# One VectorE operation in an activation, the first pair of units started beside the last single one, and other buffer counts in the merge

## Chip, cores, metric

The kernel runs on one core of a Trainium2 chip. The metric is the device time of one execution in microseconds (us); for each kernel the median of several runs is given. A profile is one execution of its own, taken with the hardware profiler. TensorE is called PE here, its weight loads PEld, VectorE DVE, ScalarE ACT, GpSimd POOL and the queue that starts most transfers SP (SPq in rows). L213 means line 213 of the kernel before.

## What is computed

One step of a hybrid decoder layer, for a prompt of 1024 tokens and for 8 samples of 4 new tokens each with 2048 past tokens in a paged cache. The part that the change touches is the compressed-block branch and what follows the attention:

```python
def compress(k, pe, w1, w2):
    # blocks of 32 positions every 16: two chunks of 16 positions make a block
    proj = jnp.einsum('bckx,mxh->mbckh', chunks, w1r)
    hid = pe.reshape(-1) @ w1
    for m in range(CMP_RATIO):
        hid = hid + proj[m, :, m:m + n_cmp]
    return jax.nn.gelu(hid) @ w2

def merge_and_mlp(x, a, c, ga, gb, w_nsa_out, w_conv_out, w_o, g_mlp, w_up, w_down):
    m = jax.nn.sigmoid(ga) * (a @ w_nsa_out) + jax.nn.sigmoid(gb) * (c @ w_conv_out)
    x = x + m @ w_o
    h = rms_norm(x, g_mlp)
    return x + jnp.square(jax.nn.relu(h @ w_up)) @ w_down
```

`compress` is applied to the keys and values of the prompt and of each of the 8 samples: 18 units. The samples' attention then uses compressed blocks, selected blocks gathered from the cache, and a window.

## The kernel before

Every product in float32 is made of three products of rounded halves (`mm3`, L212 to L215), so a tile that enters a product is first split: a cast on ACT gives the high part, a subtraction on DVE the low part. The kernel is written with a planner: each engine executes its instructions in one fixed order, which the planner derives before the run from the order of the program and from its own estimate of when each is ready. A buffer count (`bufs=`) says how many tiles of a tag live at once; a tile beyond it waits for the release of an earlier one.

The stages in order of time: projections and short convolution (to 325 us), the prompt's attention beside the gates' products (to 840 us), six single sample units among it, five pairs of sample units beside the samples' attention (865 to 1087 us), the merge of the branches (to 1172 us), the product with w_o in two halves of columns (to about 1270 us), the MLP up and down (to the end).

A single sample unit (`comp_unit`, L528) gathers its rows from the cache by a POOL transfer (`gth`), orders them by head (`gpr`, DVE, one of four quarters on POOL), transposes them on PE (`ct`), splits them (`cth`, `ctl`) and multiplies by w1 into `hid`. It stops at a first `yield`; then ACT adds the bias into the tile `x` (named gx, L592), and after a second `yield` `blocks_out` (L488) follows: Square on ACT (L492), two operations on POOL (L493, L494), Tanh on ACT (L495), one operation on DVE (L496), the product with w2 on PE (`kvc`, L513 or L519) and a copy out of PSUM (L515 or L526). `compress` (L705) starts a unit, then finishes the one before it by `finish` (L711), so that the chain of one unit lies beside the products of the next.

A pair (`pair_unit`, L646) handles two samples with shared weight sums. It has three stages of products, n = 0, 1, 2, with a `yield` after each. The loop at L1332 goes over five pairs; after stage 0 it finishes the unit before, and after each stage it advances the generator `probs`, the samples' attention, by some steps. `probs` consists of 62 steps: 21 for the softmax weights of each group of four samples (window keys `swn` transposed into `skT`, selected rows `gk` gathered on POOL, weights written to DRAM as `sl_d`), then 10 for the values of each group (weights read back into `skt`, products `so`). The step counts come from

```python
            for _ in range(SSTEP[i + n % 2] * 2 // 3):
                next(probs, None)
```

with values 6 and 7, so 4 steps after each stage, 12 for a pair. Before the loop stand, in this order, `finish()` at L1324 (the last single unit), the closing of its pools, the opening of the pools for the pairs and of another PSUM layout, and the loading of weight sums.

The merge goes over 8 tiles of 128 output channels, j = 0 to 7. For each, `load_merge` (L1291) brings the gate `ta` and the conv branch `cg` (EB buffers each), `load_wn` (L1298) the weights `wnr`, which are split into `wnh` and `wnl`. Of the split weights two slots serve j = 0, 1, 3, 4, 6, 7 and one serves j = 2, 5. `merge_in` multiplies (`na`, three column banks), adds on DVE (L1376) and POOL (L1377), and L1397, L1398 split the result (`mT`). `load_wo` (L1400) loads and splits eight tiles for each half of w_o, with WOB buffers and two raw ones (`wor`).

Of the kernel before, what the change touches and what calls it, by code (L numbers as in the profile page):

```python
# [11 lines left out]
F32 = mybir.dt.float32  # L12
# [3 lines left out]
AF = mybir.ActivationFunctionType  # L16
OP = mybir.AluOpType
# [29 lines left out]
CJ = (1, 3)  # L47
W1S = 4
UGP = 1
EB = 3  # L50
XTB = 5
ATT = dict(lg=3, pt=2, pv=1, gx=1, gy=1)
PB = 12
WOB = 9
QB = 12
WB = 2
GB = 2
# [6 lines left out]
HALVES = (slice(0, 512), slice(512, D))  # L64
QTB = 2
PTB = 2
UG = 1
TORDER = (0, 1, 2, 3, 8, 4, 5, 6, 7)
NP0 = 4
SDOWN = {**{p: (p - 1,) for p in range(1, 11)}, 11: (10, 11), 12: (12, 13), 13: (14, 15)}  # L70
WUB = 6
CB = 2
SADV = [2] * 10
SSTEP = [0, 0, 0, 0, 0, 0, 6, 6, 6, 6, 6, 6, 6, 6, 6, 7]
SKT = 5
GPRP = (3,)
GK = 4
# [43 lines left out]
def tile_hybrid_step(ctx, tc, xp, xs, cck, ccv, csk, csv, swk, swv, sconv, ptab, g_attn, w_in,  # L121
# [366 lines left out]
    def blocks_out(kv, x, t, n, b):  # L488

        prompt, nv = b is None, 2 * n - 2  # L490
        xv, tv = x[:, :, :nv], t[:, :, :nv]
        S.activation(tv, xv, AF.Square)  # L492
        P.tensor_scalar(tv, tv, 0.044715, 1.0, op0=OP.mult, op1=OP.add)  # L493
        P.tensor_mul(tv, tv, xv)  # L494
        S.activation(tv, tv, AF.Tanh, scale=GC)  # L495
        V.scalar_tensor_tensor(xv, tv, 1.0, xv, op0=OP.add, op1=OP.mult)  # L496
        xh = x.rearrange("p m (c h) -> p m c h", h=2)
        w2 = w2t[kv]
        nblk = n - 1
        po = ps(HT["ct"], "kvc")  # L500
        if kv == "k":
            if prompt:
                for h in range(2):
                    for mt in range(2):
                        PE.matmul(po[:, h * 64:h * 64 + nblk], w2[:, mt].rearrange("p a d -> p (a d)"),
                                  xh[:, mt, :nblk, h], start=mt == 0, stop=mt == 1)
                pv = po[:, :128].rearrange("p (h c) -> p h c", h=2)[:, :, :nblk]
                S.copy(pkh[:, :, :nblk], pv)
                V.tensor_sub(pkl[:, :, :nblk], pv, f32(pkh[:, :, :nblk]))
            else:  # L510
                for h in range(2):
                    for mt in range(2):
                        PE.matmul(po[h * 64:h * 64 + 64, :nblk], w2[:, mt, 0, :], xh[:, mt, :nblk, h],  # L513
                                  start=mt == 0, stop=mt == 1)
                V.tensor_copy(kcT[:, b, :], po[:, :nblk])  # L515
        else:
            for h in range(2):
                for mt in range(2):
                    PE.matmul(po[:nblk, h * 64:h * 64 + 64], xh[:, mt, :nblk, h], w2[:, mt, 0, :],  # L519
                              start=mt == 0, stop=mt == 1)  # L520
            if prompt:
                pv = po[:nblk, :128].rearrange("p (h d) -> p h d", h=2)
                S.copy(pvc[:nblk, :, 0, :], pv)
                V.tensor_sub(pvc[:nblk, :, 1, :], pv, f32(pvc[:nblk, :, 0, :]))
            else:
                V.tensor_copy(vcN[:, b, :], po[:nblk, :128])  # L526

    def comp_unit(kv, w1, cv, n, b):  # L528


        cols = 2 * n
        prompt = b is None
        hid = ps(HT["hid"], "hid")
        pieces = []
        for lp2 in range(4):
            hi = up.tile([128, 2, 256], F32R, name="cth", tag="cth", bufs=CB)
            lo = up.tile([128, 2, 256], F32R, name="ctl", tag="ctl", bufs=CB)
            pt = ps(HT["ct"], "ct")
            pv = pt[:, :2 * cols].rearrange("p (i c h) -> p i c h", i=2, h=2)
            part = cv(lp2)  # L540
            for i in range(2):
                for h in range(2):
                    PE.transpose(pv[:, i, :, h], part[:, h, i * 128:i * 128 + 128], ident[:n, :n])
            pf = pt[:, :2 * cols].rearrange("p (i c) -> p i c", i=2)
            if prompt:

                for m in range(2):
                    c = slice(m * 128, m * 128 + cols - 2)
                    src = pf[:, :, 2 * m:2 * m + cols - 2]
                    S.copy(hi[:, :, c], src)  # L550
                    V.tensor_sub(lo[:, :, c], src, f32(hi[:, :, c]))
                    c = slice(m * 128 + cols - 2, m * 128 + cols)
                    src = peT[kv][:, m * 8 + 2 * lp2:m * 8 + 2 * lp2 + 2]
                    src = src[:, :, None].to_broadcast([128, 2, 2])
                    V.tensor_copy(hi[:, :, c], src)
                    V.tensor_sub(lo[:, :, c], src, f32(hi[:, :, c]))
            else:
                S.copy(hi, pf)  # L558
                V.tensor_sub(lo, pf, f32(hi))
            pieces.append((hi, lo))  # L560
        if prompt:
            for i in range(16):
                m, lp = i % 2, i // 2
                k = m * 8 + lp
                hi, lo = (z[:, lp % 2, m * 128:m * 128 + 128] for z in pieces[lp // 2])
                PE.matmul(hid[:, :256], hi, w1[k][0], start=i == 0, stop=False)
                PE.matmul(hid[:, :256], hi, w1[k][1], start=False, stop=False)
                PE.matmul(hid[:, :256], lo, w1[k][0], start=False, stop=i == 15)
            turned = up.tile([128, 2, 256], F32, name="gx", tag="gx", bufs=UGP if prompt else UG)[:, 0]
            V.tensor_copy(turned, hid[:, :256])  # L570
            hid = ps(HT["hid"], "hid")
            hv = hid[:, :256].rearrange("p (m c) -> p m c", m=2)
            for mt in range(2):
                PE.transpose(hv[:, mt], turned[:, mt * 128:mt * 128 + 128], ident)
        else:
            hv = hid.rearrange("p (m c) -> p m c", m=2)
            nn = cols - 2
            for mt, i in MTI:
                m, lp = i % 2, i // 2
                k = m * 8 + lp  # L580
                hi, lo = (z[:, lp % 2, 2 * m:2 * m + nn] for z in pieces[lp // 2])
                ws = slice(mt * 128, mt * 128 + 128)
                mm3(hv[:, mt, :nn], w1[k][0][:, ws], w1[k][1][:, ws], hi, lo, i == 0 and mt == 0, i == 15 and mt == 1)
        yield
        pb = pbias[kv]
        if prompt:
            V.tensor_copy(pb, hv[:, :, cols - 2])
        nv = cols - 2
        x = up.tile([128, 2, 256], F32, name="gx", tag="gx", bufs=UGP if prompt else UG)
        t = up.tile([128, 2, 256], F32, name="gt", tag="gt", bufs=UGP if prompt else UG)  # L590
        for mt in range(2):
            S.activation(x[:, mt, :nv], hv[:, mt, :nv], AF.Identity, bias=pb[:, mt:mt + 1])  # L592
        yield
        blocks_out(kv, x, t, n, b)
# [51 lines left out]
    def pair_unit(kv, cache, b0, w1):  # L646
# [15 lines left out]
            xs.append(xt.rearrange("p i (j e h) -> p i j e h", e=2, h=2))  # L662
        x = u2.tile([128, 2, 512], F32, name="gx2", tag="gx2", bufs=1)
        xo = x.rearrange("p m (j e h) -> p m j e h", e=2, h=2)
        mid = u2.tile([128, 2, 256], F32, name="mid", tag="mid", bufs=1)
        pb = pbias[kv]
        for n in range(3):
            hid = ps(HT["hid"], "hid")
# [26 lines left out]
                             mid[:, :, :2 * nj].rearrange("p m (j h) -> p m j h", h=2))  # L695
        yield
        for s_ in range(2):
            t = u2.tile([128, 2, 256], F32, name="gt", tag=("gt", "mid")[s_], bufs=1)
            blocks_out(kv, x[:, :, s_ * 256:s_ * 256 + 256], t, 128, b0 + s_)

    behind = []
# [596 lines left out]
    def load_wn(j, raw=None):  # L1298

        if raw is None:  # L1300
            raw = ep.tile([128, 4, 128], F32, name="wnr", tag="wnr", bufs=1)
        DMA.dma_start(raw, w_nsa[0, :, j * 128:(j + 1) * 128].rearrange("(k p) c -> p k c", p=128))
        pool, n = (wp, 2) if j % 3 < 2 else (ep, 1)
        h, l = (pool.tile([128, 4, 128], F32R, name="wn" + x, tag="wn" + x, bufs=n) for x in "hl")
        S.copy(h, raw)
        V.tensor_sub(l, raw, f32(h))
        return h, l
# [13 lines left out]
        compress(sample_unit("k", cck, i, w1), ("k", i))  # L1321
        advance(STEP[i])
    advance(100)
    finish()  # L1324
    close("unit", "pa", "cTh")
    s1 = open_pool("s1", "right", bufs=2)
    up = u2 = open_pool("u2", "right")
# [4 lines left out]
    for i in range(ATTEND + 1, 2 * NB, 2):  # L1332
# [4 lines left out]
        for n in range(3):  # L1337
            next(unit)
            if n == 0:
                finish()  # L1340
            for _ in range(SSTEP[i + n % 2] * 2 // 3):
                next(probs, None)
            if i == 2 * NB - 2:
                if n == 0:
                    close("w2")
                    ap_ = open_pool("aT", "left")
                    aTh = ap_.tile([128, 4, T], F32R, name="aTh")
                    aTl = ap_.tile([128, 4, T], F32R, name="aTl")
                    wp = open_pool("w", "left")
                    wns = []  # L1350
                if n < 2:
                    load_aT(n)
                    wns.append(load_wn(n, room()[:, 0].rearrange("p (k c) -> p k c", k=4)))
                else:
                    for qi in (2, 3):
                        load_aT(qi)
# [492 lines left out]
```

## Time and profile before

| what | value |
|---|---|
| median of 3 runs | 1959.02 us (1954.49 to 1960.22) |
| the profiled execution, its own time | 1965.28 us |
| span of its instructions | 1963.5 us |
| PE busy | 1898.9 us, 97% |
| DVE, ACT, POOL busy | 1129.9, 859.0, 443.8 us |
| mean granted PE clock | 0.985 |

Engines work side by side, so the busy times do not add up to the span. An engine's idle time matters only where the others wait for it. The granted clock of PE is 1.0 at full speed (2.4 GHz) and 0.5 at its lower level (1.2 GHz); a stretch with a value between has a part at either.

### The profile page before, as it was taken

The numbers are of one execution on the slowest core, as the hardware profiler recorded it, in microseconds if no ns is written. First come the engines' busy times: TensorE is split into PE (matmuls) and PEld (weight loads), VectorE is DVE, ScalarE is ACT, GpSimd is POOL, SyncE is SP. The second block draws the span as 40 slices with busy tenths as digits, with TensorE's granted clock in tenths as the row PEclk, the third lists the DMA queues.
The fourth block names the chain that finished last, engine by engine and source line by source line (L and its number), as shares of the span: only waits on it lengthen the run. The fifth ranks groups of instructions, "written<-read, shape, count | busy, mean of one in ns | idle before, by whom it ended". The sixth has DMA issues, their size and how long they took to land.

```text
span 1963.5 us, 34847 instructions
## 1 busy us (share of the span) xinstructions
PE 1898.9 (97%) x13172; PEld 1766.6 (90%) x13172; DVE 1129.9 (58%) x2375; ACT 859.0 (44%) x1905; POOL 443.8 (23%) x626
## 2 busy tenths in 40 slices
PE   9999999999999999989899989999999999999998
PEld 8999998999998989876778877799999999999998
DVE  5324232454446666657775452498676755667765
ACT  5113223555546555545444230365454444443333
POOL 3112223443444444433232340130000000000000
PEclk9999999999999999989999999999999999999999
DMA  6465326222236521165536454337666656755654
GB/s 207 128 160 135 94 62 157 79 60 69 75 73 206 174 98 52 47 197 186 164 123 209 169 190 143 123 107 253 230 208 222 214 210 225 251 184 166 186 194 158
DMA packets 236312, 303.77 MB, mean 155 GB/s; under 512 B 20661, under 2 KB 163142, under 8 KB 232048
## 3 DMA queue, kind: packets, MB, share of 16 engines
q1 hardware_dynamic: 229232, 267.99, 43.9%
q0 software_dynamic: 6912, 33.56, 4.9%
q8 instruction: 104, 1.70, 0.4%
q14 instruction: 64, 0.52, 0.1%
HBM read 222.78 MB, written 78.71 MB: 154 GB/s over the span
## 4 chain that ended last, share of the span: by engine, by line
PE 70%; DMA 5%; DVE 4%; ACT 2%; POOL 1%; issue 1%; SPq 0%; DVEq 0%; POOLq 0%; ACTq 0%
PE c L213 9%; PE c L214 9%; PE c L215 9%; PE PT L942 3%; PE ga L214 3%; PE ga L213 3%; PE ga L215 3%; PE hid L214 2%; PE hid L215 2%; PE hid L213 2%; DMA wrd<-sd_d 2%; PE pv L949 2%; PE pv L948 2%; PE so L1234 1%; PE sl L1195 1%; PE skT L1103 1%
## 5 line engine op out<-in xcount | busy, mean ns | idle before, releaser
L213 PE MATMUL c<-ud,whd 128*128 128x264 f32 x768 | 218.5, 287 | 6.8 <-ACT whd L1645 4.3
L214 PE MATMUL c<-ud,whd 128*128 128x264 f32 x768 | 218.2, 286 | 0.0
L215 PE MATMUL c<-ud,whd 128*128 128x264 f32 x768 | 218.2, 286 | 0.0
L868 POOL TENSOR_SCALAR P<-P,st,gates 128x256 f32<-128x256 f32 (+4 forms) x272 | 150.2, 569 | 127.2 <-DVE st L864 104.6
L213 PEld LDWEIGHTS c<-ud,whd 128*128 128x128 f32 x768 | 145.1, 190 | 7.2 <-ACT whd L1645 4.5
L213 PE MATMUL c<-hBt,wuh 128*128 128x264 f32 x512 | 146.1, 285 | 2.3 <-ACT p L1534 2.3
L215 PE MATMUL c<-hBt,wul 128*128 128x264 f32 x512 | 146.3, 286 | 0.0
L214 PEld LDWEIGHTS c<-ud,whd 128*128 128x128 f32 x768 | 145.8, 190 | 0.0
L215 PEld LDWEIGHTS c<-ud,whd 128*128 128x128 f32 x768 | 145.1, 190 | 0.0
L946 DVE TENSOR_TENSOR ptl<-PT,pth 128x512 fp32r<-128x512 f32 (+1 forms) x148 | 99.5, 686 | 65.7 <-ACT pth L945 65.3
L1645 ACT CAST whd<-wrd 128x512 fp32r<-128x512 f32 x112 | 68.3, 621 | 152.2 <-issue 97.3
L213 PE MATMUL ga<-hTh,whu 128*128 128x384 f32 (+1 forms) x384 | 128.4, 334 | 0.0
L214 PE MATMUL ga<-hTl,whu 128*128 128x384 f32 (+1 forms) x384 | 127.0, 331 | 0.0
L215 PE MATMUL ga<-hTh,wlu 128*128 128x384 f32 (+1 forms) x384 | 126.6, 330 | 0.0
L236 POOL TENSOR_TENSOR wlu<-wru,whu 128x1024 fp32r<-128x1024 f32 x32 | 76.7, 2397 | 216.3 <-ACT whu L235 216.3
L1646 DVE TENSOR_TENSOR whd<-wrd,whd 128x512 fp32r<-128x512 f32 x112 | 76.5, 691 | 84.3 <-ACT whd L1645 84.0
L945 ACT CAST pth<-PT 128x512 fp32r<-128x512 f32 (+1 forms) x148 | 83.7, 588 | 67.8 <-PE PT L942 64.4
L214 PE MATMUL c<-h2r,wuh 128*128 128x264 f32 x384 | 109.6, 285 | 0.3 <-POOL h2r L1560 0.2
L213 PE MATMUL hid<-cth,w1h 128*128 128x254 f32 (+1 forms) x352 | 102.6, 292 | 2.7 <-ACT cth L558 1.9
L214 PE MATMUL hid<-ctl,w1h 128*128 128x254 f32 (+1 forms) x352 | 103.8, 295 | 1.4 <-DVE ctl L682 1.4
L942 PE MATMUL PT<-cst,P 128*128 128x128 f32 (+1 forms) x592 | 101.0, 274 | 0.2 <-DVE st L923 0.2
L215 PE MATMUL hid<-cth,w1l 128*128 128x254 f32 (+1 forms) x352 | 99.7, 283 | 0.0
(540 smaller groups left out, 5949.2 us busy)
## 6 DMA issues: line engine op xcount, KB each, us to landing
ur<-u_d SPq DMA_DIRECT2D x96, 264.0 KB
wru<-in_w_up SPq DMA_DIRECT2D x36, 512.0 KB
u_d<-u SPq DMA_DIRECT2D x64, 264.0 KB
wru<-in_w_in SPq DMA_DIRECT2D x32, 512.0 KB
h2r<-in_w_down SPq DMA_DIRECT2D x32, 512.0 KB
sd_d<-h2r SPq DMA_DIRECT2D x16, 1024.0 KB
wrd<-sd_d SPq DMA_DIRECT2D x64, 256.0 KB
wrd<-in_w_down SPq DMA_DIRECT2D x48, 256.0 KB
```

The source lines that it names most:

```text
L213: PE.matmul(out, wh, ah, start=first, stop=False)
L214: PE.matmul(out, wh, al, start=False, stop=False)
L215: PE.matmul(out, wl, ah, start=False, stop=last)
L236: (leng or P.tensor_sub)(l, raw, f32(h))
L868: P.tensor_scalar(p, p, self.st[:, br, 3, g:g + 1], gates[:, self.qi, 3 * hg + br:3 * hg + br + 1], op0=OP.mult, op1=OP.mult)
L942: PE.transpose(pt[:n, g * 128:(g + 1) * 128], pg[g], ident)
L945: S.copy(hi[:n], pt[:n])
L946: V.tensor_sub(lo[:n], pt[:n], f32(hi[:n]))
L948: PE.matmul(self.o, w, hi[:n], start=first and i == 0, stop=False)
L949: PE.matmul(self.o, w, lo[:n], start=False, stop=last and i == len(tiles) - 1)
L1645: S.copy(h, raw)
L1646: lows.append(V.tensor_sub(l, raw, f32(h)))
```

## The change

It makes five edits. In `blocks_out` the two POOL operations become one DVE operation, with the constants moved into the scale of Tanh; t·(1 + 0.044715·t²) is written as 0.044715·t·(t² + 1/0.044715). `finish()` ahead of the pairs becomes one step of the waiting unit, up to its second `yield`, and the unit is finished after stage 0 of the first pair; for this its tiles `gx` and `gt` move into the pool `cmp`, which stays open, and the pair's `mid` and second `gt` share them. The steps of `probs` become 5, 4 and 4 after the stages, 13 for a pair. `ta` and `cg` get four buffers in place of three, `wnr` two in place of one. The split tiles of w_o get eight in place of nine.

```diff
-EB = 3
+EB = 4
-WOB = 9
+WOB = 8
-UG = 1
-SSTEP = [0, 0, 0, 0, 0, 0, 6, 6, 6, 6, 6, 6, 6, 6, 6, 7]
+SSTEP = (5, 4, 4)
@@ blocks_out
         S.activation(tv, xv, AF.Square)
-        P.tensor_scalar(tv, tv, 0.044715, 1.0, op0=OP.mult, op1=OP.add)
-        P.tensor_mul(tv, tv, xv)
-        S.activation(tv, tv, AF.Tanh, scale=GC)
+        V.scalar_tensor_tensor(tv, tv, 1 / 0.044715, xv, op0=OP.add, op1=OP.mult)
+        S.activation(tv, tv, AF.Tanh, scale=0.044715 * GC)
@@ comp_unit
-            turned = up.tile([128, 2, 256], F32, name="gx", tag="gx", bufs=UGP if prompt else UG)[:, 0]
+            turned = up.tile([128, 2, 256], F32, name="tu", tag="tu", bufs=UGP)[:, 0]
-        x = up.tile([128, 2, 256], F32, name="gx", tag="gx", bufs=UGP if prompt else UG)
-        t = up.tile([128, 2, 256], F32, name="gt", tag="gt", bufs=UGP if prompt else UG)
+        x, t = (mp.tile([128, 2, 256], F32, name=nm, tag=nm, bufs=1) for nm in ("gx", "gt"))
@@ pair_unit
-        mid = u2.tile([128, 2, 256], F32, name="mid", tag="mid", bufs=1)
+        mid = mp.tile([128, 2, 256], F32, name="mid", tag="gx", bufs=1)
-            t = u2.tile([128, 2, 256], F32, name="gt", tag=("gt", "mid")[s_], bufs=1)
+            t = mp.tile([128, 2, 256], F32, name="gt", tag=("gt", "gx")[s_], bufs=1)
@@ load_wn
-            raw = ep.tile([128, 4, 128], F32, name="wnr", tag="wnr", bufs=1)
+            raw = ep.tile([128, 4, 128], F32, name="wnr", tag="wnr", bufs=2)
@@ ahead of the pairs
     advance(100)
-    finish()
+    next(behind[0][0])
     close("unit", "pa", "cTh")
@@ loop over the pairs
-            for _ in range(SSTEP[i + n % 2] * 2 // 3):
+            for _ in range(SSTEP[n]):
                 next(probs, None)
```

## Rows read from the trace of the kernel before

**Rows 1.** The page: busy us of each engine, share of the span, instructions.

```profile
PE 1898.9 (97%) x13172; PEld 1766.6 (90%) x13172; DVE 1129.9 (58%) x2375; ACT 859.0 (44%) x1905; POOL 443.8 (23%) x626
```

**Rows 2.** Waits of PE, 840 to 1110 us: for whom, us, times, longest.

```profile
PE kvc L513 <- DVE gx L496: 5.3, 1, 5.3
PE so L1234 <- DMA skt<-sl_d: 3.7, 1, 3.7
PE skT L1103 <- DMA swn<-in_state_win_k: 3.1, 1, 3.1
```

**Rows 3.** Waits of PE, 1110 to 1165 us.

```profile
PE na L213 <- ACT wnh L1305: 10.9, 3, 4.1
```

**Rows 4.** PE in order of time, 857 to 871 us: start, us, operation [idle before].

```profile
863.03 1.12 PE L513 MATMUL kvc<-gx,w2k 128*64 128x127 f32 x8 [5.29 <-DVE gx L496]
864.56 1.97 PE L660 MATMUL ct<-cst,gpr 128*128 128x128 f32 x8 [0.40 <-DVE kcT L515]
...
870.31 0.36 PE L213 MATMUL hid<-cth,w2h 128*128 128x256 f32 x1
```

**Rows 5.** DVE in order of time, 857 to 865 us.

```profile
858.46 0.28 DVE L515 COPY kcT<-kvc 128x127 f32<-128x127 f32 x1
```

**Rows 6.** Seven stretches: length, busy us per engine, granted PE clock, DMA share, GB/s.

```profile
864.15:870.31 6.16, 5.76 (x46) 5.24 (x45) 3.75 (x12) 2.52 (x5) 2.68 (x8) 0.55 1.01 349
1114.82:1118.41 3.59, 0.00 (x0) 0.00 (x1) 3.54 (x9) 2.70 (x7) 2.26 (x2) 1.00 0.00 0
...
1129.26:1132.47 3.21, 0.00 (x1) 0.00 (x1) 2.21 (x4) 2.09 (x4) 0.24 (x1) 1.00 0.39 130
1132.47:1136.00 3.53, 3.53 (x12) 3.47 (x13) 3.53 (x6) 1.68 (x4) 2.23 (x2) 0.52 0.60 194
1145.91:1149.98 4.07, 0.01 (x1) 0.00 (x1) 2.90 (x7) 1.66 (x3) 2.65 (x3) 0.94 1.06 391
1149.98:1153.00 3.02, 3.02 (x10) 3.02 (x11) 1.40 (x2) 0.45 (x1) 0.43 (x1) 0.51 0.70 251
...
1050.17:1057.40 7.23, 7.23 (x36) 6.33 (x38) 1.53 (x4) 0.39 (x1) 0.00 (x0) 0.53 0.08 24
```

**Rows 7.** Two lines of the kernel: operation, count, ns min/median/max, start of first and last.

```profile
L494 POOL TENSOR_TENSOR gt<-gt,gx x18: 730/1275/1594, 213.6 to 1094.5; 128x508 f32<-128x508 f32 x16, 128x252 f32<-128x252 f32 x2
L496 DVE SCALAR_TENSOR_TENSOR gx<-gt,gx x18: 422/680/1158, 214.8 to 1098.0; 128x508 f32<-128x508 f32 x16, 128x252 f32<-128x252 f32 x2
```

**Rows 8.** Stages of pairs and of w_o's turn: length, PE, PEld, DVE, ACT, POOL busy, clock, DMA.

```profile
870.50:1087.00 216.50, 206.55 (x1463) 162.46 (x1461) 151.10 (x282) 101.75 (x192) 70.26 (x67) 0.98 0.55 177
...
1216.90:1237.40 20.50, 19.40 (x81) 14.40 (x80) 9.38 (x12) 5.40 (x9) 1.70 (x4) 1.00 0.35 109
```

**Rows 9.** DVE and POOL in order of time, 912 to 919 us.

```profile
915.69 2.17 DVE L481 TENSOR_TENSOR w1l<-w1r,w1h 128x512 fp32r<-128x512 f32 x1
...
918.12 0.68 DVE L481 TENSOR_TENSOR w1l<-w1r,w1h 128x512 fp32r<-128x512 f32 x1
...
916.03 1.28 POOL L494 TENSOR_TENSOR gt<-gt,gx 128x508 f32<-128x508 f32 x1
```

**Rows 10.** The SP queue in order of time, 1100 to 1141 us: start and length of issues.

```profile
1101.48 1.69 SPq L1404 DMA_DIRECT2D wor<-in_w_o  x2
1119.41 0.38 SPq L1302 DMA_DIRECT2D wnr<-in_w_nsa_out  x1
...
1140.40 0.60 SPq L1302 DMA_DIRECT2D wnr<-in_w_nsa_out  x1
```

**Rows 11.** ACT in order of time, 1114 to 1150 us.

```profile
1114.90 0.52 ACT L1397 ACTIVATE mT0h<-ta 128x384 fp32r<-128x384 f32 x1 [18.48 <-PE ownT L1256]
...
1149.31 0.62 ACT L1305 CAST wnh<-wnr 128x512 fp32r<-128x512 f32 x1 [0.25 <-DVE ta L1376]
```

**Rows 12.** ACT in order of time, 1213 to 1220 us.

```profile
1213.69 1.14 ACT L1407 CAST woh<-wor 128x512 fp32r<-128x512 f32 x2 [41.71 <-PE wo L226]
1218.22 1.27 ACT L1407 CAST woh<-wor 128x512 fp32r<-128x512 f32 x2 [3.39 <-DMA wor<-in_w_o]
```

## Prediction

> **What bounds the kernel now.** First the page: PE is busy for 1898.9 of 1963.5 us [rows 1]. DVE, the next engine, is busy 58% of the span. So only two things shorten this kernel: PE standing idle for less time, or PE running for less time at its lower clock. The change takes no product away. The next view is therefore PE's waits over the stages that the change touches. From 840 to 1110 us, which holds the last single unit and the five pairs, three waits matter: 5.3 us for the activation chain of the last single unit, 3.7 us for a weight read back from DRAM, and 3.1 us for a window tile [rows 2]. In the merge there are three waits of 10.9 us together, all for the split of `wnh` [rows 3]; in order of time they are 3.59, 3.21 and 4.07 us, as the stretches without PE in [rows 6] show. The last view is the granted clock just behind such waits. It is 0.51 to 0.55 for the next 3 to 7 us [rows 6], the lower level for nearly all of the stretch, and a wait costs that as well: 3.53 x 0.48 = 1.7 us in the stretch from 1132.47 us, 3.02 x 0.49 = 1.5 us from 1149.98 us, 7.23 x 0.47 = 3.4 us from 1050.17 us.
>
> **The unit finished behind stage 0.** Now PE has nothing to do between the last single unit's products and its `kvc`, which start at 863.03 us after 5.29 us of waiting; the first transposes of the pair (`ct`) stand behind them in PE's fixed order and start at 864.56, the pair's first products (`hid`) at 870.31 us [rows 4]. In the changed order `ct` comes first. What it still needs is the PSUM bank that the unit before used, free when the copy L515 ends at 858.46 + 0.28 = 858.74 us [rows 5]; its data had been ordered by head before that. So `ct` should start near 858.8 in place of 864.56 us, 5.8 us earlier. The eight `kvc` products are not gone, they come back behind stage 0 with up to the 1.1 us that they took [rows 4]. Term: 5.8 - 1.1 = 4.7 us gained. Bounds: 0, if the loading of the weight sums is late next; and 5.29 + 0.40 + 6.16 x 0.45 = 8.5 us, if the stretch at clock 0.55 [rows 6] also runs at full speed and nothing else does its waiting. The moved chain adds a wait: `mid` shares its buffer with the unit's `gx`, so the bias on ACT (L692) waits for `kvc`, and behind it on ACT queue the casts `cth` for stage 1, for which PE waits. At most that is the same 1.1 us, once. The unit issues no transfers after its start, so none is moved. On POOL's queue the first four gathers of `gk` stand behind L494 of this unit; without it they can go sooner, and no wait of PE is put down to them [rows 2].
>
> **The activation.** It goes over 18 units. POOL loses two operations in each, the larger with a median of 1.275 us [rows 7]; POOL is busy for 70.3 of 216.5 us in the pairs [rows 8] and bounds nothing there. DVE gains one operation of a form and size that it already runs in L496, median 0.680 us [rows 7]: 16 x 0.68 + 2 x 0.42 = 11.7 us over the kernel, of which ten, 6.8 us, lie in the pairs. There DVE is busy for 151.1 of 216.5 us [rows 8] and would rise from 70 to 73%. The price is on the path where the new operation, waiting for Square on ACT, stands ahead of a `ctl` on DVE's queue for which PE waits. Bounds: 6.8 us lost, if each of the ten delays PE by its full length; and 0.6 us gained, the difference once, since the chain itself is shorter (at least 1.28 us of POOL against 0.68 of DVE, and the 10 chains overlap other work). I take 1 us lost: DVE is idle for over a quarter of the stage, and PE's queue there has other work ready.
>
> What speaks for less: where L494 runs on POOL, a DVE subtraction beside it took 2.17 us and the same form without it 0.68 us [rows 9]. The Trainium skill, SBUF — State Buffer, Who interferes with whom, says that a DVE instruction with two inputs in SBUF blocks fully against a POOL instruction that reads SBUF, whichever starts second. The trace agrees. The same rule also speaks against the edit, since the new operation has two such inputs and can itself be held by POOL's remaining work; by it the term would be nearer to 0 than to 1 us lost.
>
> **The steps of probs.** No work is added: the steps that do something stay 62, and they come up to five earlier in program order at the end of the pairs. What can change is what PE meets in its queue. The 3.7 us wait is for a transfer of weights, the 3.1 us wait for a window tile [rows 2], both transfers of SP whose place in the order moves. Bounds: both waits and their clock gone, 3.7 + 3.1 + 3.4 + 1.6 = 11.8 us (1.6 as in the other short waits); or as much again added. I take 0, because the length of those transfers and the number of their buffers stay.
>
> **Four merge tiles, two raw weight buffers.** The load of `wnr` for j = 3 is issued at 1119.41 us, when the split of j = 2 has freed the one raw buffer; SP had issued its last load ahead of it by 1103.17 [rows 10]. PE's wait of 3.21 us for its cast ends at 1132.47 us [rows 3, 6]. With a second buffer the load can follow the others at about 1102, 17 us sooner. What is late next is the slot for the split tile, which j = 0 leaves when its last bank is multiplied. PE's last products before the wait end at 1129.26 us [rows 6], and j = 1 and 2 each have a bank after that of j = 0, so the slot is free a few us before it is needed. For j = 5 the load goes at 1140.40 us [rows 10], the cast at 1149.31 [rows 11], and the wait is 4.07 us [rows 6]; its load stands on SP's queue behind loads of `ta` and `cg` that wait for one of three buffers, and the fourth buffer lets those go a tile sooner. Both gone: 3.21 + 4.07 + 1.7 + 1.5 = 10.5 us, with the clock from above. The first wait, 3.59 us, stays: its cast stands on ACT behind `mT`, which had waited 18.48 us until 1114.90 [rows 11], and no buffer count changes that. Bounds: 0, if the casts keep their places in ACT's order behind `mT`; 10.5 + 3.59 + 1.6 = 15.7 us, if the planner also turns the first. I take 9.
>
> **Eight tiles of w_o.** With nine, one tile of the second half of w_o is split ahead of time; with eight all wait for the last products of the first half. The casts then go in twos, the second two 4.5 us after the first [rows 12]. PE is idle for 1.1 of 20.5 us there now [rows 8]. One more tile late is half of such a turn, 2.3 us, part of it covered by the products of three row blocks that are open at once. Bounds: 0 and 4.5; I take 1.5 us lost.
>
> **Sum.** -4.7 + 1.0 + 0 - 9.0 + 1.5 = -11.2 us. The profiled execution took 1965.28 us (span 1963.5) and would take 1954.1; it lies 6.3 us above the median of the runs. From that median, 1959.02 - 11.2 = 1947.8, so 1948 us.
>
> **Rivals.** A measurement of this kernel can tell about 0.3%, 6 us, from no change: under 1953 is faster, above 1965 slower.
> (1) Forecast: the chain at the first pair and two of three waits of the merge go. 1948, its own range 1939 to 1955. 0.60.
> (2) The merge keeps its waits: the casts stay behind `mT` and the loads of w_o on ACT, and the earlier landing is worth nothing. For it: the first of the three waits is already of that kind [rows 11]. Against: the load of j = 3 starts only at 1119.41. Then -4.7 + 1.0 + 1.5 = -2.2, 1957 us. 0.18.
> (3) Slower: the denser steps put products of `probs` that wait for a transfer ahead of the pairs' own on PE's fixed queue, in each pair instead of in two of the five. Three more such waits of 3.4 us with 2.5 us of clock are 17.7 us, the sum is +6.5 and the time 1965.5. It decides from two such added waits on. For it: both waits there now are of this kind [rows 2]. Against: most steps find their data. 0.10.
> (4) More: the planner's new order also removes the first wait of the merge (5.2 us) and one of the two in the pairs (about 6): -22, 1937 us. 0.12.
> The range from 1935 to 1960 holds (1), (2), and most of (4). Chances: faster 0.69 (nearly all of (1), and (4)), same 0.20 ((2) and the rest of (1)), slower 0.11.
>
> **What the profile after would show.** `ct` of the first pair within 2 us behind the last single unit's products, and `kvc` of that unit behind the 48 products of the pair's stage 0, with no wait for L496. No L493 or L494 work on POOL. `wnr` for j = 3 issued right behind the first three pairs of `ta` and `cg`, and one wait of PE for `wnh` in place of three, with clock 1.0 from 1120 us on. In w_o, eight casts after the last product of the first half. I am wrong if waits for `ctl` appear in each pair, if the pairs' stage (216.5 us, less what the first pair gains) grows, or if the casts of `wnh` still stand behind `mT`.

## The result and the profile after

The changed kernel takes 1941.98 us (median of 6 runs, 1940.09 to 1948.32), the kernel before 1959.62 us (6 runs, 1954.49 to 1965.02). The ratio is 0.9917, with a 95% interval of 0.9894 to 0.9940: 16.3 us less, between 11.8 and 20.8. The forecast was 11.2 us less, 1948 us. The time lies in the range and the direction is right, but three of the five terms behind it are not (the first pair, the steps of `probs` and the tiles of w_o), as the runs below show.

The profiled execution of the changed kernel took 1940.09 us, its lowest time, and that of before 1965.28 us, above all six runs counted here. The two traces are therefore 25.2 us apart where the medians are 17.6 apart. Sizes of stages are read from the traces, verdicts from the ratios.

The page of the changed kernel, answering to [rows 1]:

```profile
PE 1885.6 (97%) x13172; PEld 1753.9 (91%) x13172; DVE 1132.3 (58%) x2393; ACT 857.6 (44%) x1905; POOL 412.3 (21%) x590
```

PE runs the same 13172 products in 13.3 us less: it spends less time at the lower clock. DVE has 18 instructions more, POOL 36 fewer. Cutting both spans at the same products shows where the 25.2 us lie. The marks are the prompt's last product `pv`, the first pair's first transpose `ct`, and the last `hid`, `na` and `wo`.

| stretch | before, us | after, us | difference |
|---|---|---|---|
| to the last `pv` (attention) | 840.3 | 839.1 | -1.2 |
| to the first `ct` of the pairs (last single unit) | 24.2 | 21.4 | -2.8 |
| to the last `hid` (five pairs) | 222.6 | 209.9 | -12.7 |
| to the last `na` (merge) | 82.9 | 74.9 | -8.0 |
| to the last `wo` (first half of w_o) | 47.0 | 47.5 | +0.5 |
| to the last `dn` (second half of w_o, MLP) | 738.9 | 737.9 | -1.0 |

The pairs gave most, where I had forecast nothing. The granted clock tells how. Stages of the kernel before, then of the changed one (length, busy us of PE, PEld, DVE, ACT, POOL, PE clock, DMA share, GB/s):

```profile
864.56:1087.11 222.55, 212.60 (x1506) 167.99 (x1507) 154.57 (x293) 104.46 (x196) 72.67 (x75) 0.97 0.56 182
1087.11:1170.05 82.94, 71.32 (x438) 65.72 (x437) 42.97 (x79) 23.02 (x45) 31.60 (x30) 0.94 0.53 184
```

```profile
860.52:865.40 4.88, 4.88 (x38) 4.35 (x39) 2.67 (x8) 2.93 (x7) 0.00 (x0) 0.53 0.96 269
866.23:1070.44 204.21, 198.85 (x1438) 155.10 (x1437) 155.45 (x294) 103.23 (x194) 53.42 (x49) 1.00 0.56 178
1070.44:1145.39 74.95, 70.97 (x468) 65.35 (x467) 43.31 (x84) 20.76 (x41) 28.39 (x27) 0.98 0.63 219
```

From 866 us to the end of the pairs PE now runs at full clock. DVE is busy for 155.45 of 204.21 us, 76% (the forecast had 73%), and that costs little. The waits of PE, 840 to 1110 us and then the merge (for whom, us, times, longest), answering to [rows 2, 3]:

```profile
PE ct L657 <- DVE kcT L513: 6.2, 1, 6.2
PE hid L213 <- DVE ctl L679: 4.1, 6, 1.1
...
PE na L212 <- ACT wnh L1302: 3.1, 1, 3.1
```

Three things are seen. Both waits for transfers in the pairs are gone, 3.1 us for `swn` and 3.7 us for `skt`. The merge has one wait for `wnh` in place of three. And the wait at the first pair has not gone: it was 5.3 us of `kvc` for `gx`, and is 6.2 us of `ct` for `kcT`.

**The first pair.** PE in order of time in the changed kernel (start, us, operation, idle before), answering to [rows 4]:

```profile
853.66 0.68 PE L511 MATMUL kvc<-gx,w2k 128*64 128x127 f32 x8
860.52 0.69 PE L657 MATMUL ct<-cst,gpr 128*128 128x128 f32 x2 [6.19 <-DVE kcT L513]
...
873.88 0.68 PE L511 MATMUL kvc<-gx,w2k 128*64 128x127 f32 x8
```

The order is the one forecast: `ct` comes first, and the last single unit's `kvc` follows among the pair's products, at full clock. But `ct` starts 6.19 us after the products before it (854.33 us), where before it started 6.8 us after them (857.74 to 864.56). DVE's queue shows why:

```profile
856.65 0.42 DVE L473 TENSOR_TENSOR both<-w1r 128x256 f32<-128x256 f32 x1 [2.12 <-DMA w1r<-in_cmp_w_k]
...
859.85 0.43 DVE L473 TENSOR_TENSOR both<-w1r 128x256 f32<-128x256 f32 x1 [0.64 <-DMA w1r<-in_cmp_w_k]
860.19 0.28 DVE L513 COPY kcT<-kvc 128x127 f32<-128x127 f32 x1
```

The copy that frees the PSUM bank takes 0.28 us and could run at 854.4. It stands right behind the seventh of eight sums of weights (`both`), and these wait for their loads. In the kernel before it stands at the same place, as in every kernel here whose sums run on DVE; there the seventh sum came 0.4 us after the products, and the copy behind it [rows 5]:

```profile
858.12 0.43 DVE L474 TENSOR_TENSOR both<-w1r 128x256 f32<-128x256 f32 x1 [0.45 <-DMA w1r<-in_cmp_w_k]
```

So it is not DVE's order that changed here. Measured from the last `pv`, the products end 2.2 us sooner (15.2 us after it, before 17.4) and the seventh sum starts 2.9 us later (20.7, before 17.8). Its loads are slower. SP and POOL in the kernel before, then in the changed one:

```profile
846.61 10.56 SPq L470 DMA_DIRECT2D w1r<-in_cmp_w_k  x6
861.75 1.00 POOL L621 DMA_INDIRECT gk<-in_cache_slc_k,idx  x1 [0.15 <-issue]
```

```profile
842.87 15.84 SPq L469 DMA_DIRECT2D w1r<-in_cmp_w_k  x6
843.47 1.19 POOL L618 DMA_INDIRECT gk<-in_cache_slc_k,idx  x1 [0.30 <-issue]
```

SP issues the loads of `w1r` as the sums free their buffers: six took 10.56 us before and take 15.84 us now. What is new beside them are the first four gathers of `gk`, which had stood on POOL's queue behind L494 of the last single unit. The forecast saw that they can go sooner and put nothing down for it. In the seven kernels of this document whose gathers start before 851 us, the third of these loads takes 5.8 to 7.6 us from its issue to its sum, in the seven others 2.8 to 3.1 us. No run moved the gathers alone, so that they are the cause is argued from these rows and not shown by an experiment.

**The merge.** SP and ACT in the changed kernel, answering to [rows 10, 11]:

```profile
1089.28 0.52 SPq L1299 DMA_DIRECT2D wnr<-in_w_nsa_out  x1
...
1092.30 11.23 SPq L1299 DMA_DIRECT2D wnr<-in_w_nsa_out  x2
```

```profile
1097.19 0.62 ACT L1302 CAST wnh<-wnr 128x512 fp32r<-128x512 f32 x1 [15.49 <-DMA wnr<-in_w_nsa_out]
1102.98 0.52 ACT L1394 ACTIVATE mT0h<-ta 128x384 fp32r<-128x384 f32 x1 [5.18 <-PE ownT L1253]
...
1112.27 0.62 ACT L1404 CAST woh<-wor 128x512 fp32r<-128x512 f32 x1 [2.06 <-DMA wor<-in_w_o]
...
1114.14 1.14 ACT L1302 CAST wnh<-wnr 128x512 fp32r<-128x512 f32 x2
```

The load for j = 3 goes 3 us behind that for j = 2, as forecast. The cast for j = 2 now stands ahead of `mT`, so the first wait, which I had held to stay, is gone. The wait that stays is that of j = 3; its cast, and that of j = 4 with it, stands behind casts of `woh` that wait for loads of w_o.

### The profile page after: what moved, and what is told of

Read it like the earlier page. It is cut to its first block, busy times and chain, and to the rows that moved or that the text cites. A ratio compares the mean times of both kernels' runs of the same rounds, so it can differ in the third digit from the quotient of the medians.

```text
span 1938.0 us, 34844 instructions
## 1 busy us (share of the span) xinstructions
PE 1885.6 (97%) x13172; PEld 1753.9 (91%) x13172; DVE 1132.3 (58%) x2393; ACT 857.6 (44%) x1905; POOL 412.3 (21%) x590
## 4 chain that ended last, share of the span: by engine, by line
PE 84%; DMA 6%; DVE 4%; issue 3%; ACT 1%; POOL 1%; SPq 1%; DVEq 0%; POOLq 0%; ACTq 0%
PE c L213 9%; PE c L212 9%; PE c L214 9%; PE PT L939 3%; PE ga L213 3%; PE ga L212 3%; PE ga L214 3%; PE hid L213 2%; PE hid L214 2%; PE hid L212 2%; DMA wrd<-sd_d 2%; PE pv L946 2%; PE pv L945 2%; PE sl L1192 2%; PE so L1231 1%
## 5 line engine op out<-in xcount | busy, mean ns | idle before, releaser
L235 POOL TENSOR_TENSOR wlu<-wru,whu 128x1024 fp32r<-128x1024 f32 x32 | 76.8, 2399 | 222.6 <-ACT whu L234 222.6
L212 PEld LDWEIGHTS c<-hBt,wuh 128*128 128x128 f32 x512 | 97.4, 191 | 2.9 <-ACT hBt L1553 2.6
```

The costliest lines, as they stand in the source:

```text
L212: PE.matmul(out, wh, ah, start=first, stop=False)
L235: (leng or P.tensor_sub)(l, raw, f32(h))
```

## The experiments

Microseconds are the ratio taken from 1959.6 us, with its interval. The stretches are cut from each kernel's trace as in the table above.

| kernel | ratio | us less | last unit | pairs | merge |
|---|---|---|---|---|---|
| before | 1 | 0 | 24.2 | 222.6 | 82.9 |
| changed | 0.9917 (0.9894 to 0.9940) | 16.3 | 21.4 | 209.9 | 74.9 |
| a1: first pair alone | 0.9966 (0.9951 to 0.9982) | 6.7 | 22.8 | 214.5 | 83.3 |
| a2: activation alone | 0.9946 (0.9924 to 0.9967) | 10.6 | 26.4 | 206.1 | 80.2 |
| a3: steps alone | 0.9936 (0.9919 to 0.9953) | 12.5 | 24.2 | 207.9 | 83.5 |
| a4: buffers alone | 0.9952 (0.9933 to 0.9971) | 9.4 | 24.5 | 223.2 | 71.0 |
| b1: changed, old steps | 0.9915 (0.9900 to 0.9931) | 16.7 | 21.5 | 209.9 | 75.6 |
| b2: changed, old activation | 0.9906 (0.9889 to 0.9923) | 18.4 | 22.8 | 206.7 | 74.1 |
| b3: changed, old first pair | 0.9932 (0.9915 to 0.9950) | 13.3 | 26.5 | 208.4 | 72.8 |
| b4: before, steps 5, 4, 3 | 0.9977 (0.9962 to 0.9992) | 4.5 | 24.8 | 212.5 | 86.2 |
| c1: changed, sums on POOL | 0.9886 (0.9867 to 0.9904) | 22.3 | 16.7 | 210.7 | 74.0 |
| c2: changed, splits put earlier in the program | 0.9921 (0.9903 to 0.9938) | 15.5 | 21.3 | 210.8 | 74.6 |
| c3: before, two `wnr` | 0.9969 (0.9956 to 0.9983) | 6.1 | 24.8 | 218.1 | 74.7 |
| d1: c1, splits on POOL | 0.9887 (0.9852 to 0.9922) | 22.1 | 16.7 | 209.8 | 81.0 |

Some products of `na` and `so` lie on either side of the mark between pairs and merge (1473 matmul records in the pairs of a2, 1506 in those of before), so a few us between those two columns are a shift and no gain.

**Each part alone (a1 to a4).** On the kernel before, one part each of the change shown above.

```diff
a1 -    finish()
   +    next(behind[0][0])          (with gx, gt and mid in the pool cmp)
a2 -        P.tensor_scalar(...); P.tensor_mul(...)
   +        V.scalar_tensor_tensor(tv, tv, 1 / 0.044715, xv, op0=OP.add, op1=OP.mult)
a3 -            for _ in range(SSTEP[i + n % 2] * 2 // 3):
   +            for _ in range(SSTEP[n]):            (SSTEP = (5, 4, 4))
a4 -EB = 3, WOB = 9, wnr bufs=1
   +EB = 4, WOB = 8, wnr bufs=2
```

> Only the order at the first pair is changed: the last single unit is finished behind the pair's stage 0, its tiles lie in the pool that stays open. Theory A (the forecast's step): ct of the first pair starts within 2 us behind the last single unit's products, 4.7 us less, about 1955 if before is 1959.6. Theory B (the trace of after, where ct waits 6.19 us for the copy of kcT that stands on DVE behind sums of weights): the wait keeps its length with another cause, the gain is 0 to 1.5 us, 1958 to 1960.

> Only the activation is changed, one DVE operation for two of POOL. Forecast's step: 1 us lost, between 0.6 gained and 6.8 lost; 1959 to 1966, waits of PE for ctl in the pairs grow from 2.3 us by less than 7. Rival: POOL's operations had held DVE up, and without them the pairs run shorter by some us (1953 to 1957), with DVE's subtractions w1l of 2.17 us gone.

> Only the steps of probs are changed, 5, 4 and 4 for a pair in place of 4, 4 and 4. Theory A: this alone takes away both waits for transfers in the pairs (3.1 us for swn, 3.7 us for skt) with their clock, 8 to 12 us less, 1948 to 1952. Theory B (the forecast's value): nothing, 1957 to 1962; the waits go only with the other edits, by a new order of the planner.

> Only the buffers are changed: four ta and cg, two wnr, eight split tiles of w_o. Theory A (forecast): the second and third wait for wnh go, the first stays; 9 us less in the merge, up to 1.5 lost at w_o: 1950 to 1953. Theory B: casts keep their places in ACT's order and the waits stay: 1957 to 1962.

Alone they give 6.7, 10.6, 12.5 and 9.4 us, 39.2 in sum; together 16.3. So 23 us of the single gains are the same gain counted more than once. The waits of PE say which. First a4, then a1, a2 and a3:

```profile
PE skT L1103 <- DMA swn<-in_state_win_k: 3.7, 1, 3.7
PE so L1234 <- DMA skt<-sl_d: 3.6, 1, 3.6
PE na L213 <- ACT wnh L1305: 3.5, 1, 3.5
```

```profile
PE ct L659 <- DVE kcT L515: 6.2, 1, 6.2
```

```profile
PE kvc L512 <- DVE gx L495: 8.5, 1, 8.5
...
PE so L1233 <- DMA skt<-sl_d: 1.4, 1, 1.4
```

```profile
PE kvc L513 <- DVE gx L496: 5.3, 1, 5.3
...
PE so L1234 <- DMA skt<-sl_d: 0.4, 1, 0.4
```

Only a4 keeps both waits for transfers, and its pairs take as long as before (223.2 us). Up to the merge its instructions stand in the order of before on every engine. Each of the other three gives the pairs another order, and in each the two waits are gone or nearly so, and the pairs are 8.1, 16.5 and 14.7 us shorter. Three edits that have little in common take away the same waits. (a1 and a2 share one thing, the gathers of `gk` that go sooner; in a3 they go at 858.65 us, as late as in before, and the pairs are as short.)

For a1, theory B is right about the place (`ct` waits 6.2 us for `kcT`) and wrong about the time, which comes from the pairs. For a2, the forecast's step fails: 10.6 us less in place of 1 us more. The rival, POOL holding DVE up, had the direction, but a3 keeps POOL's operations and its pairs are as short. At the first pair the edit does cost something, since the wait of `kvc` grows from 5.3 to 8.5 us. The operation stands on DVE behind the same sums, and their loads are late here too, beside gathers that start at 849.58 us: the eighth sum starts 22.0 us after the last `pv`, in before 19.6 us:

```profile
867.25 0.42 DVE L474 TENSOR_TENSOR both<-w1r 128x256 f32<-128x256 f32 x1 [0.94 <-DMA w1r<-in_cmp_w_k]
...
867.92 0.68 DVE L493 SCALAR_TENSOR_TENSOR gt<-gt,gx 128x508 f32<-128x508 f32 x1
```

For a3, theory A holds. For a4, theory A holds to the letter: the first wait of the merge stays with 3.5 us, the other two are gone.

**Each part undone (b1 to b3).** On the changed kernel, one part set back, by the same lines in reverse.

```diff
b1 -            for _ in range(SSTEP[n]):
   +            for _ in range(SSTEP[i + n % 2] * 2 // 3):
b2 -        V.scalar_tensor_tensor(tv, tv, 1 / 0.044715, xv, ...)
   +        P.tensor_scalar(...); P.tensor_mul(...)
b3 -    next(behind[0][0])
   +    finish()
```

> The changed kernel with the steps of probs as before, 4, 4 and 4. Alone on the kernel before, the steps gave 12.5 us. Theory S (shared waits: each of three edits alone removes the same two waits for transfers in the pairs, by a new order of the planner, so the gain is had once): within 4 us of the changed kernel, 1938 to 1946, and no wait for swn or skt in the pairs above 1.5 us. Theory A (each edit has its own gain): 12.5 us are lost, 1954.

> The changed kernel with the two operations on POOL as before. Alone the new activation gave 10.6 us. Theory S (shared waits): within 4 us of the changed kernel, 1938 to 1946. Theory C (POOL's operations held DVE up through the pairs, and without them each pair is shorter): 8 to 10 us are lost, 1950 to 1952.

> The changed kernel with the last single unit finished ahead of the pairs, as before. Alone the new order gave 6.7 us, none of it at the first pair, where ct waited 6.2 us for a copy. Theory S: within 4 us of the changed kernel, with a wait of 5 to 8.5 us of kvc for gx in place of that of ct for the copy. Theory D (the new order is worth its own time there): 4.7 us lost, 1947.

The waits of b1, then of b3:

```profile
PE ct L657 <- DVE kcT L513: 6.7, 1, 6.7
```

```profile
PE kvc L512 <- DVE gx L495: 8.7, 1, 8.7
...
PE so L1233 <- DMA skt<-sl_d: 0.9, 1, 0.9
PE skT L1102 <- DMA swn<-in_state_win_k: 0.8, 1, 0.8
```

Theory S holds. Without the steps, which alone were worth 12.5 us, the time is the same (0.9915 against 0.9917). Without the activation, which alone was worth 10.6 us, it is no longer either (0.9906); theory C, 8 to 10 us lost, is out. Without the new first pair it is 3 us longer (0.9932), with intervals that overlap, so that S and D can't be told apart by the time. By the trace, b3's last unit takes 26.5 us against 21.4, with a wait of 8.7 us at the place where a2 has 8.5. The buffers of the merge were not set back in the changed kernel.

b2 also answers the question of POOL and DVE. DVE's subtraction `w1l`, in before and in b2 (count, ns min/median/max):

```profile
L481 DVE TENSOR_TENSOR w1l<-w1r,w1h x32: 674/691/2175, 161.3 to 931.7; 128x512 fp32r<-128x512 f32 x32
```

```profile
L480 DVE TENSOR_TENSOR w1l<-w1r,w1h x32: 674/686/696, 161.3 to 930.8; 128x512 fp32r<-128x512 f32 x32
```

The 2.17 us of [rows 9] are gone in b2 too, although POOL's operations are still there; in the changed kernel, without them, the longest is 0.97 us. Whether the two meet is a matter of order. By the Trainium skill (SBUF — State Buffer, Who interferes with whom) such a DVE instruction contends with a POOL instruction that reads SBUF, and the order of issue decides which is held. The row of before agrees in the length alone: the subtraction, which starts first (915.69 us), is the long one, and POOL's product beside it (916.03 us) takes 1.28 us, its median. No difference in time between the kernels is shown to come from it.

**Does any new order do it? (b4).** The kernel before with the same 12 steps for a pair, one of them a stage earlier.

```diff
-SSTEP = [...]     (4, 4 and 4 steps)
+SSTEP = (5, 4, 3)
```

> The kernel before with 5, 4 and 3 steps in a pair in place of 4, 4 and 4: the same 12 steps for a pair, one of them a stage earlier, so that hardly anything but the planner's order changes. Theory P (any new order may lose the two waits): one or both of the waits of 3.1 and 3.7 us are gone, 4 to 12 us less than before. Theory N (it takes more steps for a pair, so that transfers come earlier): both waits stay, within 4 us of before.

```profile
PE na L213 <- ACT wnh L1305: 11.2, 3, 4.5
...
PE so L1234 <- DMA skt<-sl_d: 2.7, 1, 2.7
```

The wait for `swn` is gone and that for `skt` is 2.7 us in place of 3.7; the time is 4.5 us less (1.6 to 7.4), at the near end of theory P. By the time alone theory N is not ruled out; by SP's queue it is, where both loads now go ahead of the writes shown below. More steps aren't needed for a gain. The SP queue of the kernel before, then of the changed one, shows the difference for `swn` (start, length of issues):

```profile
954.91 0.38 SPq L1128 DMA_DIRECT2D swn<-in_state_win_k  x1
957.64 0.39 SPq L1088 DMA_DIRECT2D out<-swn  x1
958.08 0.38 SPq L1089 DMA_DIRECT2D out<-swn  x1
958.55 0.40 SPq L1128 DMA_DIRECT2D swn<-in_state_win_k  x1
```

```profile
953.50 2.62 SPq L1125 DMA_DIRECT2D swn<-in_state_win_k  x2
960.23 0.38 SPq L1085 DMA_DIRECT2D out<-swn  x1
```

Before, two writes of the first tile stand between the two loads, and the second load can't go before the first has landed. In the changed kernel both loads go first. Of all the kernels here only before, a4, b3 and c3 have writes between these two loads; there PE waits 3.1, 3.7, 0.8 and 0 us, in the ten others not at all. For `skt` the traces show no such turn of the queue. In before 6.5 us lie between the issue of the first read-back (1043.71 us) and the product that takes it (1050.17), in the changed kernel 5.9 us (1039.20 to 1045.14), and there PE has other products in between. Why it has more to do meanwhile isn't shown further than that its order is another.

**What keeps the first pair's gain away? (c1).** The changed kernel with the sums added and split on POOL.

```diff
-                V.tensor_add(both, raw[:, 0], raw[:, 1])
+                E = V if parts else P
+                E.tensor_add(both, raw[:, 0], raw[:, 1])
                 S.copy(h, both)
-                V.tensor_sub(l, both, f32(h))
+                E.tensor_sub(l, both, f32(h))
```

> The changed kernel with the sums of weights that are loaded ahead of the first pair added and split on POOL in place of DVE, so that the copy of kcT, for which ct waits 6.2 us, no longer stands on DVE's queue behind operations that wait for loads of w1r. Theory Q (that queue is what kept the first pair's gain away): ct starts within 2 us behind the last single unit's products, 4 to 6 us less than the changed kernel, 1936 to 1938. Theory R (the loads themselves are late next): the wait moves to the first products of the pair, hid for w2h, and the time stays within 2 us, 1940 to 1944.

DVE, then PE:

```profile
857.77 0.29 DVE L514 COPY kcT<-kvc 128x127 f32<-128x127 f32 x1 [4.90 <-PE kvc L512]
```

```profile
857.04 0.68 PE L512 MATMUL kvc<-gx,w2k 128*64 128x127 f32 x8
858.12 1.09 PE L658 MATMUL ct<-cst,gpr 128*128 128x128 f32 x8 [0.41 <-DVE kcT L514]
...
862.77 0.66 PE L1101 MATMUL skT<-cst,swn 128*128 128x128 f32 x4 [2.37 <-DMA swn<-in_state_win_k]
```

Theory Q holds: `ct` starts 0.41 us behind the products, the last unit takes 16.7 us in place of 21.4, and the time is 1937.72 us (1936.90 to 1939.53). That is 4.3 us less than the changed kernel (1940.09 to 1948.32, no run in common, though the intervals of the two ratios overlap), and the fastest median here. But c1 changes two things. POOL now has the sums ahead of the gathers, which go from 857.85 us on, and the third load of `w1r` takes 2.8 us again. So the copy's place behind the sums and the slow loads are both gone, and c1 doesn't tell what either is worth alone; theory R was not tested with the loads as slow as in the changed kernel. Next late is a window tile, 2.4 us and 0.8 us, which is a load and not an order on DVE.

**The last wait of the merge (c2, d1).** c2 puts the split for j + 3 into the program right behind the last bank of j; d1 takes c1 and gives the splits for j from 2 on to POOL.

```diff
c2 +            if i == 2 and len(wns) < 8:
   +                wns.append(load_wn(len(wns)))
d1 -        S.copy(h, raw); V.tensor_sub(l, raw, f32(h))
   +        P.tensor_copy(h, raw); P.tensor_sub(l, raw, f32(h))      (j >= 2)
```

> The changed kernel with the split of w_nsa_out for j + 3 put into the program right behind the last bank of j, in place of a place two tiles later behind other work. The remaining wait of the merge, 3.1 us for wnh of j = 3, stands on ACT's queue behind casts of woh that wait for their loads. Theory E (that order is the cause): the wait goes with its clock, 4 to 5 us less, 1937 to 1938. Theory F (the slot of j = 0 is the bound): the wait stays, 1941 to 1943.

> The kernel with the sums on POOL (1937.7 us, wait of 4.0 us for wnh in the merge), and in it the split of w_nsa_out for j = 2 to 7 on POOL in place of ACT and DVE, so that it no longer stands behind the splits of the merge and the casts of woh on ACT's queue. Theory E (ACT's order keeps the last wait of the merge): the wait goes, 4 us and up to 1.7 of clock, 1932 to 1934. Theory G (a POOL split takes longer and stands behind the additions ta of the same queue, which wait for PE in turn): new waits of PE for wnh or wnl, two of 3 us or more, 1940 to 1946.

c2's wait for `wnh` is 2.6 us and its casts for j = 3 and 4 still stand behind four casts of `woh` on ACT: the planner gave them the same place, so the edit did not do what it says and decides nothing between E and F. PE, DVE, ACT and POOL have the order of the changed kernel throughout, and on SP's queue one load of `wnr` goes two places earlier. So c2 is nearly a second measurement of the changed kernel, 15.5 us less after 16.3; c1, measured in the same series, is 7.4 us below it (1937.72 and 1945.09 us, no run in common).

In c1 the wait that is left is not that of j = 3, which is 0.3 us, but again that of j = 2, 4.0 us, its cast behind `mT` as in before. In d1 the wait is for POOL:

```profile
PE na L212 <- POOL wnh L1307: 3.8, 1, 3.8
...
PE na L214 <- POOL wnl L1308: 1.6, 1, 1.6
```

Theory G: the split now stands on POOL's queue behind the additions of `ta`. The merge takes 81.0 us in place of 74.0, part of which the first half of w_o gives back (43.2 us after 47.5), and the time is that of c1. What bounds the last wait stays open; a queue with nothing late on it was not found.

**One raw buffer more, alone (c3).**

```diff
-            raw = ep.tile([128, 4, 128], F32, name="wnr", tag="wnr", bufs=1)
+            raw = ep.tile([128, 4, 128], F32, name="wnr", tag="wnr", bufs=2)
```

> The kernel before with the second raw buffer for the weights alone (three ta and cg, nine split tiles of w_o as before). The forecast's step gives this buffer the wait of j = 3 (3.2 us with 1.7 of clock) and the fourth buffer of ta and cg that of j = 5 (4.1 with 1.5): 4.9 us less, about 1954 where all three buffers gave 9.4. Rival: the raw buffer carries both, 9 us less, 1950.

```profile
PE na L213 <- ACT wnh L1305: 5.4, 2, 3.6
```

The merge shrinks from 82.9 to 74.7 us by this buffer alone, of 71.0 with all three. The waits are 3.60 us for j = 2 and 1.83 us for j = 3; that of j = 5 is gone. So the wait of j = 5 did not need the fourth buffer of `ta` and `cg`. The time, 6.1 us less, lies nearer to the forecast's 4.9 than to the rival's 9. What is left for j = 3 has the form seen in the changed kernel:

```profile
1127.58 0.60 ACT L1407 CAST woh<-wor 128x512 fp32r<-128x512 f32 x1
1128.08 1.14 ACT L1305 CAST wnh<-wnr 128x512 fp32r<-128x512 f32 x2
```

## Why the prediction was right or wrong

**First pair, 4.7 us: wrong by its mechanism.** The step said that the bank of `ct` is free when the copy L515 ends, and took that copy's time from before. It named the case in which the term is 0, the loading of the weight sums being late next, and did not follow it: the copy is an instruction on DVE that stands behind seven of those sums, in before as in the changed kernel, and it can't come sooner than their loads. These came later than before, beside the gathers that the step had let go sooner without a price. Gained at this place were 6.8 - 6.2 = 0.6 us, and 0.4 us in the `kvc` products, which take 0.68 us at full clock in place of 1.12. The other 2.2 of the 2.8 us in the table lie ahead of this place and are not of this step: in before PE waits 1.42 us for `cth` early in the unit and runs at clock 0.57 from 842 to 846 us, in the changed kernel its longest wait there is 0.75 us and the clock is 1.00 from 840 to 848 us. The 1.42 us are in all seven kernels without the new activation, the 0.75 us in all seven with it. With the sums off DVE's queue and the loads in time again (c1) the stretch is 4.7 us shorter than in the changed kernel, so the term's size could be had, but not by this edit.

**Activation, 1.0 us lost: not wrong in the sum, but wrong for the edit alone.** With the other parts in place it is worth nothing that can be told (0.9917 with it, 0.9906 without). Alone it gained 10.6 us, through the order of the pairs. The waits for `ctl`, which the step feared, are 4.1 us after 2.3, in the first two pairs alone, well inside the bound of 6.8.

**Steps of probs, 0: the step that failed.** Its bounds, 11.8 us to either side, came from the right two waits and their clock, and the measured value for the edit alone, 12.5 us (9.2 to 15.9), is at the end of them. I took 0 because the length of the transfers and the number of their buffers stay. What decides is the order in which loads, writes and products stand in the queues, and three of the five edits change it. For `swn` SP's rows show how; for `skt` it stays open. Rival (4) had this as one wait of the two, with a chance of 0.12; both went.

**Merge, 9.0 us: right in size, half right in its reasons.** Alone the buffers gave 9.4 us (5.7 to 13.1), the second and third wait went and the first stayed (a4). But the second raw buffer gave most of that, and it also took the wait of j = 5 (c3), which the step had put down to the fourth buffer of `ta` and `cg`. In the changed kernel the first wait is gone and that of j = 3 has come back, so "no buffer count changes that" was too much: the cast for j = 2 had only to come ahead of `mT`.

**Eight tiles of w_o, 1.5 us lost: wrong in sign.** The loss was to lie at the turn to the second half. In the first 20.5 us there PE is idle for 0.2 us, in before for 1.1 us [rows 8], and in no kernel with eight tiles for longer than in before. The 0.5 us of the first half of w_o lie at another place, and c3, which has nine tiles, shows them too (47.5 us).

**The sum.** By the traces: last unit -2.8 (forecast -4.7), pairs -12.7 (+1.0), merge -8.0 (-9.0), the first half of w_o +0.5 and what follows its turn -1.0 (+1.5). That the sum came near is in part luck: what the first pair did not give, the pairs gave several times over. The range held because it reached towards rival (4), which with its 1937 us is about as near to 1942 as the forecast's 1948. The slower rival (3), products of `probs` that wait for transfers, saw the right place with the wrong sign.

## What to carry to other kernels

Where a planner derives the order of the queues, measure each part of a change both alone and left out: parts that gave 39 us one by one gave 16 together, because three of them removed the same two waits. Before a wait is booked as gone, list what stands ahead, on its own engine's queue, of the instruction that releases it: here a copy of 0.28 us stood behind sums that waited for loads, and PE waited 6.2 us for it. A transfer that an edit lets go sooner belongs into the sum as well: here gathers came to lie beside those loads. A wait whose length hangs on queue order alone has a large bound on the side of gain as well, and should not be entered as 0 because nothing in the transfer changes.

## What the runs showed that was not expected

The wait for `swn` also depends on the execution. In before, a4 and c3 the instructions stand in the same order up to the merge, and PE waited 3.1, 3.7 and 0 us for it; the wait for `skt` was 3.6 to 3.7 us in all three. So part of a trace's gain in the pairs can be chance, and c3's 218.1 us there after 222.6 is no effect of its buffer.

In the same way the stretch to the last `pv`, in which before, a3, a4, b4 and c3 run the same work, took 835.6 to 842.1 us in their five profiled executions. In a stretch of that length a difference of some 6 us between two single traces says nothing.
